# Weight sums of the seven-block products made for two chunks at once, in double-width raw tiles

## The chip, the cores and the metric

The kernel runs on one core of a Trainium2 chip. The metric is the device time of one execution in microseconds (us), as the median of several runs; the profile is one more execution of the same program, taken by the hardware profiler.

## The reference

Two pre-norm residual layers over 512 tokens of width 1024, in float32. Layer 0 has two parallel head groups (grouped-query attention A with per-head normalised and rotated queries and keys, and latent attention B), layer 1 a neighbourhood attention with a relative position bias. A squared-ReLU MLP (1024 to 4096 to 1024) follows each of them.

```python
def hybrid_attention(h, w_in, a_q_norm, a_k_norm, b_q_norm, b_w_uq, b_kv_norm, b_w_ukv, w_out, row, col):
    z = h @ w_in
    qa, ka, va, cq, ckv, kr = jnp.split(z, EVEN_SPLITS, axis=-1)
    qa = axial_rope(rmsnorm(qa.reshape(b, s, A_HEADS, HEAD_DIM), a_q_norm), row, col)
...
    oa = block_attention(qa, ka, va, HEAD_DIM ** -0.5)
    qb = (rmsnorm(cq, b_q_norm) @ b_w_uq).reshape(b, s, B_HEADS, B_NOPE + B_ROPE)
...
    kvb = (rmsnorm(ckv, b_kv_norm) @ b_w_ukv).reshape(b, s, B_HEADS, B_NOPE + B_V)
...
    return mixed @ w_out

def sq_relu_mlp(h, w_up, w_down):
    u = jax.nn.relu(h @ w_up)
    return (u * u) @ w_down
```

## The kernel before, in words

Every product is made of 128 x 128 weight blocks held still in TensorE (PE) while 256 or 512 token columns stream past. A float32 weight is split in two parts, hi (a rounded copy) and lo (the rest), and a product is the sum of three matmuls: hi with the activations' hi, hi with their lo, lo with their hi (lines 515 to 517 for plain products).

**Seven-block products.** Most of the MLPs' up product and part of their down product use a Strassen-like scheme: a 256 x 256 weight square (two k-blocks by two column blocks, 256 KB) is turned into seven 128-wide blocks, and seven half-width products (256 token columns each, three matmuls each, lines 388 to 390) take the place of eight. `seven_chunk` (line 295) makes one such chunk. It takes a free `Slot` of the big pool if more than `reserve` are free, or else one of four raw tiles of 128 x 1024; SP issues one DMA (line 300) into the first 512 columns; GpSimd (POOL) makes three sums (lines 302 to 304) in the columns 512 to 1024; after a `yield`, ScalarE (ACT) copies 896 columns to hi (line 308) and VectorE (DVE) makes lo (line 309). `Seven.plan` asks for the chunks of one group of output columns, and `Seven.run` issues their 21 matmuls each and evacuates four banks (lines 398 to 401, DVE).

**Plain chunks.** `chunk` (line 183) takes one of the four raw tiles, SP loads it (line 190, or 193 for several pieces), ACT makes hi (lines 212 or 222) and DVE or, where `eng` says so, POOL makes lo (line 202). Sweeps of the last layer (`sweep_chunk`, line 288) also fall back to these raw tiles.

**Order.** `weights(i)` keeps chunks loading up to five ahead (`LOAD`) and hi and lo made up to two ahead (`AHEAD`), in the order in which they were asked for. Tiles of a pool tag are handed out in turn, and the one who takes a tile waits for its last reader. A scheduler lays each engine's instructions in an order of its own, which is fixed before the program runs; each engine, and SP's queue of DMAs, goes through its list in order and waits at the head.

**The rope in layer 0's attention.** `rope(..., far=True)` (line 566) swaps partitions with eight DMAs on SP (line 572), multiplies by the cosines and sines on POOL (lines 576, 577), and `sum_q` (line 640) adds both on DVE (line 645), makes hi on ACT (line 647) and lo on DVE (line 648), and issues three more DMAs on SP (lines 649 to 651). Heads' scores (PE, line 1039) wait for these. Beside them run transposes (line 1014) with their copies on ACT and DVE (lines 1016, 1017) and the products with the values (line 1027).

**Bias rows.** `bias_rows` (line 1260) writes the position bias for layer 1 to DRAM: eight loads (line 1264), memsets and copies on POOL (lines 1267 to 1271), and 48 stores on SP (lines 1276, 1280, 1282). It runs as idle work beside the first seven-block stage.

Of the kernel before, what the change touches and what calls it, by code (L numbers as in the profile page):

```python
# [8 lines left out]
F32 = mybir.dt.float32  # L9
# [3 lines left out]
ALU = mybir.AluOpType  # L13
# [5 lines left out]
P = 128  # L19
# [11 lines left out]
def f32(ap):  # L31
    return ap.bitcast(F32)
# [3 lines left out]
def encoder_kernel(ctx: ExitStack, tc: tile.TileContext, ins, out, dbg=None):  # L36
    nc = tc.nc
    PE, ACT, DVE, POOL, SP = nc.tensor, nc.scalar, nc.vector, nc.gpsimd, nc.sync

    big = ctx.enter_context(tc.tile_pool(name="big", bufs=1))  # L40
    wp = ctx.enter_context(tc.tile_pool(name="wp", bufs=3))
# [7 lines left out]
    free = list(range(NSLOT))  # L49
# [11 lines left out]
    def nm(s):  # L61
        cnt[0] += 1
        return f"{s}_{cnt[0]}"
# [116 lines left out]
        return got[0]  # L180


    def chunk(parts, nk, ncol, heads=None, eng=None, first=False):

        raw = wp.tile([P, 1024], F32, tag="raw", bufs=4, name=nm("raw"))
        r3 = raw[:, 0 : nk * ncol].rearrange("p (k n) -> p k n", k=nk)
        for lo, n, src in parts:
            dst = r3[:, :, lo : lo + n]
            if len(src.shape) == 3:
                SP.dma_start(dst, src)  # L190
            else:
                for k in range(nk):
                    SP.dma_start(dst[:, k].rearrange("p (z m) -> p z m", z=src.shape[2]), src[:, k])
        yield
        hi = wp.tile([P, 1024], F32R, tag="whi", name=nm("whi"))
        lo_ = wp.tile([P, 1024], F32R, tag="wlo", name=nm("wlo"))
        m = nk * ncol
        v = lambda t: t[:, 0:m].rearrange("p (k n) -> p k n", k=nk)
        lows = []

        def low(to, src, high):
            z = lambda: (eng or DVE).tensor_tensor(to, src, f32(high), op=ALU.subtract)  # L202
            if eng:
                z()
            else:
                lows.append(z)

        if heads is None:
            if first:
                DVE.tensor_copy(hi[:, 0:m], raw[:, 0:m])  # L210
            else:
                ACT.activation(hi[:, 0:m], raw[:, 0:m], AF.Copy)  # L212
            low(lo_[:, 0:m], raw[:, 0:m], hi[:, 0:m])
        else:

            na, nb = heads
            hn = ncol // (na + nb)
            r4 = r3.rearrange("p k (h e) -> p k h e", h=hn)
            for e0, n, o in ((0, na, 0), (na, nb, hn * na)):
                z = [v(t)[:, :, o : o + hn * n].rearrange("p k (h e) -> p k h e", h=hn) for t in (hi, lo_)]  # L220
                src = r4[:, :, :, e0 : e0 + n]
                ACT.activation(z[0], src, AF.Copy)
                low(z[1], src, z[0])
        yield v(hi), v(lo_), lows

    def rows(w, k0, nk):
        return w[k0 * P : (k0 + nk) * P, :].rearrange("(k p) n -> p k n", p=P)
# [5 lines left out]
    def plan(*spec, make=None):  # L233
        asked.append((make or chunk, spec))
        return len(asked) - 1
# [56 lines left out]

    reserve = [1]

    def seven_chunk(w, k0, c0):


        slot = Slot(F32) if len(free) > reserve[0] else None
        raw = slot.t if slot else wp.tile([P, 1024], F32, tag="raw", bufs=4, name=nm("raw"))
        SP.dma_start(raw[:, 0:512].rearrange("p (k n) -> p k n", k=2), rows(w, k0, 2)[:, :, c0 : c0 + 256])  # L300
        r = raw.rearrange("p (b n) -> p b n", n=P)
        POOL.tensor_tensor(r[:, 6], r[:, 0], r[:, 1], op=ALU.subtract)  # L302
        POOL.tensor_tensor(r[:, 4:6], r[:, 2:3].to_broadcast([P, 2, P]), r[:, 0:7:6], op=ALU.add)  # L303
        POOL.tensor_tensor(r[:, 7], r[:, 3], r[:, 5], op=ALU.subtract)  # L304
        yield
        hi = wp.tile([P, 1024], F32R, tag="whi", name=nm("whi"))
        lo = wp.tile([P, 1024], F32R, tag="wlo", name=nm("wlo"))
        ACT.activation(hi[:, 0:896], raw[:, 128:1024], AF.Copy)  # L308
        DVE.tensor_tensor(lo[:, 0:896], raw[:, 128:1024], f32(hi[:, 0:896]), op=ALU.subtract)  # L309
        if slot:  # L310
            slot.free()
        yield hi, lo, []

    class Seven:
# [56 lines left out]
                s_.free()  # L371

        def plan(self, w, c0, k0=0):
            return [plan(w, k0 + 2 * kp, c0, make=seven_chunk) for kp in range(self.np)]

        def run(self, ids, evac):

# [38 lines left out]
    def product(w, k0, xk, cols, evac, banks=None, kstep=2, stride=None, eng=None, order=None):  # L416
# [13 lines left out]
        for kk in range(0, nk, kstep):  # L430
            n = min(kstep, nk - kk)
            if len(runs) > 1 and stride:
                src = w[(k0 + kk) * P : (k0 + kk + n) * P, :].rearrange("(k p) (z m) -> p k z m", p=P, m=stride)
                parts = [(0, ncols, src[:, :, 0 : len(runs), runs[0][1] : runs[0][1] + runs[0][2]])]
            else:
                src = rows(w, k0 + kk, n)
                parts = [(o, m, src[:, :, c : c + m]) for o, c, m in runs]
            ids.append(plan(parts, n, ncols, None, eng))
# [294 lines left out]
    def load_w(k):  # L733
        _, (hi, lo, lows) = chunk([(0, 768, rows(w_in, k, 1)[:, :, 0:768])], 1, 768, first=k == 0)
        for z in lows:
            z()
        W[k] = hi, lo
# [142 lines left out]
    def projB(g, last):  # L880
        Q, K, V = (QKV[g][z] for z in "QKV")
        iq = [plan([(0, 384, rows(w_uq, 0, 2)[:, :, 384 * g : 384 * g + 384])], 2, 384, (64, 32), POOL),
              plan([(0, 384, rows(w_uq, 2, 1)[:, :, 384 * g : 384 * g + 384])], 1, 384, (64, 32), POOL)]
        iv = plan([(0, 512, rows(w_ukv, 0, 2)[:, :, 512 * g : 512 * g + 512])], 2, 512, (64, 64), POOL)

# [402 lines left out]
    def sweep_chunk(w, k0, kind, made):  # L1288

        def raw():  # L1290
            slot = Slot(F32) if len(free) > reserve[0] else None
            return slot, slot.t if slot else wp.tile([P, 1024], F32, tag="raw", bufs=4, name=nm("raw"))

        def half(k, f):
            return w[k * P : (k + 1) * P, S * f : S * f + S]

        sa, a = raw()
        sb, b = raw() if kind == 2 else (None, None)
        if kind == 0:
            for z in range(2):  # L1300
                SP.dma_start(a[:, S * z : S * z + S], half(k0 + z, 0))
        else:
            for z in range(2):
                SP.dma_start(a[:, S * z : S * z + S], made(z, (z, 1 - z)[kind - 1]))
        if kind == 2:
            SP.dma_start(b[:, 0:S], half(k0 + 1, 1))
        yield
        hi = wp.tile([P, 1024], F32R, tag="whi", name=nm("whi"))
        lo = wp.tile([P, 1024], F32R, tag="wlo", name=nm("wlo"))
        ACT.activation(hi, a, AF.Copy)  # L1310
        DVE.tensor_tensor(lo, a, f32(hi), op=ALU.subtract)
        third = None
        if kind == 2:
            third = Slot()
            ACT.activation(third.t[:, 0:S], b[:, 0:S], AF.Copy)
            DVE.tensor_tensor(third.t[:, S:], b[:, 0:S], f32(third.t[:, 0:S]), op=ALU.subtract)
        for s_ in (sa, sb):
            if s_:
                s_.free()
        yield (hi, lo, third), None, []  # L1320
# [690 lines left out]
```

## Time and profile before

| what | value |
|---|---|
| median of 3 runs | 1179.63 us (1177.93 to 1180.22) |
| the profiled execution's own time | 1178.83 us |
| its span, first to last instruction | 1176.9 us |
| mean granted TensorE clock | 0.998 |
| busy: PE, DVE, ACT, POOL | 1150.5, 902.3, 655.6, 514.1 us |

Every duration below comes from the one profiled execution. "L302" is line 302 of the kernel before. A row of the timeline gives start, duration, engine, line, operation, output and inputs, and in brackets the idle time before it with what ended it. Rows of DMA issues (SPq) give the time that SP was busy with issuing, not that of the transfer. The names in_ev and in_od are weights of layer 0 and of layer 1, in_ffn those of both MLPs; raw, whi, wlo are the tiles of a chunk. "a" is a slot of the big pool, "sc" a scratch tile.

### The profile page before, as it was taken

How to read it: one execution, taken by the hardware profiler on the slowest of the kernel's cores; microseconds unless marked ns; L12 is line 12 of the kernel's file. 1: busy time of each engine (PE TensorE's matmuls, PEld its weight loads, DVE VectorE, ACT ScalarE, POOL GpSimd, SP SyncE). 2: the span in 40 equal slices, each digit the busy share in tenths (PEclk: the TensorE clock that was granted, in tenths of full speed). 3: DMA queues.
4: the chain of work that ended last, by engine and by line, in shares of the span. 5: the costliest groups of instructions: out<-in, count | busy, mean ns of one | idle time of the engine just before them, and what ended most of it. 6: DMA issues, size and time to landing. Idle time of an engine off the chain costs nothing.

```text
span 1176.9 us, 20495 instructions
## 1 busy us (share of the span) xinstructions
PE 1150.5 (98%) x7380; PEld 1024.7 (87%) x7380; DVE 902.3 (77%) x1565; ACT 655.6 (56%) x1116; POOL 514.1 (44%) x658
## 2 busy tenths in 40 slices
PE   9988999999999999999999999999999999999997
PEld 8657778888889899998998989988888999999995
DVE  4788998888977458878795676666898887699855
ACT  5467676664526246672463555555562666676625
POOL 3267444223682376828911333332179998300000
PEclk9999999999999999999999999999999999999999
DMA  7234344433645853435536775655345323375802
GB/s 245 66 94 127 87 126 106 137 79 110 184 130 134 257 177 98 135 101 163 160 72 163 185 172 150 167 146 147 119 109 161 90 82 91 99 250 172 268 1 72
DMA packets 120117, 159.78 MB, mean 136 GB/s; under 512 B 10884, under 2 KB 84529, under 8 KB 119665
## 3 DMA queue, kind: packets, MB, share of 16 engines
q1 hardware_dynamic: 109920, 127.95, 36.0%
q0 software_dynamic: 8640, 17.85, 8.9%
q10 hardware_dynamic: 1456, 12.69, 3.4%
q8 instruction: 58, 0.95, 0.3%
q14 instruction: 43, 0.34, 0.1%
HBM read 136.03 MB, written 29.36 MB: 141 GB/s over the span
## 4 chain that ended last, share of the span: by engine, by line
PE 82%; DVE 4%; ACT 1%; issue 1%; POOL 0%; DVEq 0%; ACTq 0%; POOLq 0%
PE mm L515 7%; PE mm L516 7%; PE mm L517 7%; PE mm L390 3%; PE mm L389 3%; PE mm L388 3%; PE t L389 2%; PE t L388 2%; PE t L390 2%; PE s L516 2%; PE s L517 2%; PE s L515 2%; PE s L390 2%; PE s L388 2%; PE s L389 2%; PE s L1039 1%
## 5 line engine op out<-in xcount | busy, mean ns | idle before, releaser
L309 DVE TENSOR_TENSOR wlo<-a,whi 128x896 fp32r<-128x896 f32 x116 | 149.3, 1291 | 63.0 <-ACT whi L308 62.4
L308 ACT ACTIVATE whi<-a 128x896 fp32r<-128x896 f32 x116 | 109.8, 949 | 127.1 <-PE o L516 41.3
L515 PE MATMUL mm<-a,whi 128*128 128x512 f32 x443 | 178.7, 405 | 0.6 <-DVE a L957 0.4
L517 PE MATMUL mm<-a,wlo 128*128 128x512 f32 x443 | 174.5, 395 | 0.4 <-DVE wlo L202 0.3
L516 PE MATMUL mm<-a,whi 128*128 128x512 f32 x443 | 174.6, 394 | 0.0
L202 DVE TENSOR_TENSOR wlo<-raw,whi 128x1024 fp32r<-128x1024 f32 (+4 forms) x103 | 122.7, 1195 | 48.3 <-ACT whi L212 45.9
L212 ACT ACTIVATE whi<-raw 128x1024 fp32r<-128x1024 f32 (+3 forms) x106 | 101.4, 959 | 86.8 <-PE s L516 29.4
L302 POOL TENSOR_TENSOR a<-a 128x128 f32<-128x128 f32 x116 | 76.8, 665 | 98.4 <-DMA a<-in_ffn_w_up_dram 73.0
L304 POOL TENSOR_TENSOR a<-a 128x128 f32<-128x128 f32 x116 | 106.7, 922 | 8.9
L303 POOL TENSOR_TENSOR a<-a 128x256 f32<-128x256 f32 x116 | 97.4, 843 | 8.9
L517 PEld LDWEIGHTS mm<-a,wlo 128*128 128x128 f32 x443 | 83.1, 188 | 19.5 <-DVE wlo L202 1.1
L515 PEld LDWEIGHTS mm<-a,whi 128*128 128x128 f32 x443 | 83.3, 188 | 18.1 <-DVE hT L973 0.6
L516 PEld LDWEIGHTS mm<-a,whi 128*128 128x128 f32 x443 | 83.5, 188 | 15.1
L390 PE MATMUL mm<-a,wlo 128*128 128x256 f32 x330 | 92.7, 281 | 0.0
L389 PE MATMUL mm<-a,whi 128*128 128x256 f32 x330 | 92.6, 281 | 0.0
L388 PE MATMUL mm<-a,whi 128*128 128x256 f32 x330 | 92.5, 280 | 0.0
L1047 POOL TENSOR_SCALAR p<-p,ti 128x512 f32<-128x512 f32 x64 | 46.9, 735 | 88.0 <-DVE ti L1046 68.9
L1709 POOL TENSOR_SCALAR p<-p,ti 128x256 f32<-128x256 f32 x64 | 35.5, 566 | 97.8 <-DVE ti L1708 85.6
L389 PE MATMUL t<-a,whi 128*128 128x256 f32 x232 | 65.2, 281 | 0.0
L388 PE MATMUL t<-a,whi 128*128 128x256 f32 x232 | 65.1, 281 | 0.0
L390 PE MATMUL t<-a,wlo 128*128 128x256 f32 x232 | 65.0, 280 | 0.0
L390 PEld LDWEIGHTS mm<-a,wlo 128*128 128x128 f32 x330 | 62.1, 188 | 0.3 <-DVE wlo L309 0.2
(403 smaller groups left out, 3566.1 us busy)
## 6 DMA issues: line engine op xcount, KB each, us to landing
a<-in_ffn_w_up_dram SPq DMA_DIRECT2D x101, 256.0 KB
raw<-in_ffn_w_down_dram SPq DMA_DIRECT2D x32, 512.0 KB
made<-in_ffn_w_down_dram ACTq DMA_DIRECT2D x22, 512.0 KB
a<-made SPq DMA_DIRECT2D x38, 256.0 KB
raw<-in_od_w_qkv_dram SPq DMA_DIRECT2D x64, 128.0 KB
a<-in_ffn_w_down_dram SPq DMA_DIRECT2D x29, 256.0 KB
raw<-in_ffn_w_up_dram SPq DMA_DIRECT2D x12, 512.0 KB
raw<-in_ffn_w_down_dram SPq DMA_DIRECT2D x24, 256.0 KB
```

Source lines behind the costliest of these rows:

```text
L202: z = lambda: (eng or DVE).tensor_tensor(to, src, f32(high), op=ALU.subtract)
L212: ACT.activation(hi[:, 0:m], raw[:, 0:m], AF.Copy)
L303: POOL.tensor_tensor(r[:, 4:6], r[:, 2:3].to_broadcast([P, 2, P]), r[:, 0:7:6], op=ALU.add)
L304: POOL.tensor_tensor(r[:, 7], r[:, 3], r[:, 5], op=ALU.subtract)
L308: ACT.activation(hi[:, 0:896], raw[:, 128:1024], AF.Copy)
L309: DVE.tensor_tensor(lo[:, 0:896], raw[:, 128:1024], f32(hi[:, 0:896]), op=ALU.subtract)
L388: PE.matmul(o, wh, x[:, 0], start=kp == 0 and n in (0, 1, 3, 5), stop=False, skip_group_check=True)
L389: PE.matmul(o, wh, x[:, 1], start=False, stop=False, skip_group_check=True)
L390: PE.matmul(o, wl, x[:, 0], start=False, stop=kp == self.np - 1, skip_group_check=True)
L515: PE.matmul(o, wh, xh, start=first, stop=False)
L516: PE.matmul(o, wh, xl, start=False, stop=False)
L517: PE.matmul(o, wl, xh, start=False, stop=last)
```

## The change

Two things change in how raw tiles are used. The ring of four raw tiles of 128 x 1024 becomes one of three of 128 x 2048. A pair of seven-block chunks shares one: at its first chunk both DMAs are issued, and the three sums are made for both at once, at 2 x 128, 2 x 256 and 2 x 128 columns; hi and lo are still made per chunk. Seven-block chunks no longer use slots. Where a plan has five chunks (the down product of layer 0's MLP), the pairs are 2, 2 and 1. Plain chunks and the sweeps' fall-back take halves of such tiles (six halves for four tiles); a half left over is given up when a pair begins. The scratch for DMAs that POOL issues is halved to 8192 bytes to make room.

There are 124 seven-block chunks; their 372 sums become 64 x 3 = 192 (60 for two chunks, 4 for one). The numbers of PE's, DVE's, ACT's and SP's compute instructions and transfers stay as they are.

```diff
+    spare = []
+
+    def raw_pair():
+        return wp.tile([P, 2048], F32, tag="raw", bufs=3, name=nm("raw"))
+
+    def raw_half():
+        if not spare:
+            t = raw_pair()
+            spare.extend((t[:, 0:1024], t[:, 1024:2048]))
+        return spare.pop(0)
+
     def chunk(parts, nk, ncol, heads=None, eng=None, first=False):
-        raw = wp.tile([P, 1024], F32, tag="raw", bufs=4, name=nm("raw"))
+        raw = raw_half()
...
-    def seven_chunk(w, k0, c0):
-        slot = Slot(F32) if len(free) > reserve[0] else None
-        raw = slot.t if slot else wp.tile([P, 1024], F32, tag="raw", bufs=4, name=nm("raw"))
-        SP.dma_start(raw[:, 0:512].rearrange("p (k n) -> p k n", k=2), rows(w, k0, 2)[:, :, c0 : c0 + 256])
-        r = raw.rearrange("p (b n) -> p b n", n=P)
-        POOL.tensor_tensor(r[:, 6], r[:, 0], r[:, 1], op=ALU.subtract)
-        POOL.tensor_tensor(r[:, 4:6], r[:, 2:3].to_broadcast([P, 2, P]), r[:, 0:7:6], op=ALU.add)
-        POOL.tensor_tensor(r[:, 7], r[:, 3], r[:, 5], op=ALU.subtract)
+    def seven_chunk(w, k0, c0, n, z, box):
+        if z == 0:
+            spare.clear()
+            box.append(raw_pair())
+            for q in range(n):
+                SP.dma_start(box[0][:, 1024 * q : 1024 * q + 512].rearrange("p (k n) -> p k n", k=2),
+                             rows(w, k0 + 2 * q, 2)[:, :, c0 : c0 + 256])
+            r = box[0][:, 0 : 1024 * n].rearrange("p (q b n) -> p q b n", q=n, n=P)
+            POOL.tensor_tensor(r[:, :, 6], r[:, :, 0], r[:, :, 1], op=ALU.subtract)
+            POOL.tensor_tensor(r[:, :, 4:6], r[:, :, 2:3].to_broadcast([P, n, 2, P]), r[:, :, 0:7:6], op=ALU.add)
+            POOL.tensor_tensor(r[:, :, 7], r[:, :, 3], r[:, :, 5], op=ALU.subtract)
         yield
+        raw = box[0][:, 1024 * z : 1024 * z + 1024]
...
-            return [plan(w, k0 + 2 * kp, c0, make=seven_chunk) for kp in range(self.np)]
+            boxes = [[] for _ in range(0, self.np, 2)]
+            return [plan(w, k0 + 4 * (kp // 2), c0, min(2, self.np - 2 * (kp // 2)), kp % 2, boxes[kp // 2],
+                         make=seven_chunk) for kp in range(self.np)]
...
-            return slot, slot.t if slot else wp.tile([P, 1024], F32, tag="raw", bufs=4, name=nm("raw"))
+            return slot, slot.t if slot else raw_half()
...
-    nc = _bacc.Bacc("TRN2", target_bir_lowering=False, num_devices=1)
+    nc = _bacc.Bacc("TRN2", target_bir_lowering=False, num_devices=1, dynamic_dma_scratch_size=8192)
```

Since the tiles are handed out otherwise, the scheduler lays the engines' lists otherwise. (Line numbers after are 11 to 14 higher for the same instruction.) In the seven-block stages PE's order is the same; it differs in layer 0's attention, at about 99 to 128 us. SP's list there before: the three DMAs of one query tile's rope (L649 to L651), a plain chunk of w_ukv, the eight swaps of the next tile (L572), a chunk of w_out, then the next three.

```order
L649 DMA a_622<-a_622 64x512
L650 DMA a_622<-sc_746 64x512
L651 DMA a_622<-sc_746 64x512
L190 DMA raw_1059<-in_ev_b_w_ukv_dram 128x2x512
L572 DMA sc_872<-a_126 16x512 x8
L190 DMA raw_1890<-in_ev_w_out_dram 128x2x384
L649 DMA a_871<-a_871 64x512
L650 DMA a_871<-sc_1037 64x512
L651 DMA a_871<-sc_1037 64x512
```

The same place after, with the lines 201, 586 and 663 to 665 for 190, 572 and 649 to 651:

```order
L201 DMA raw_893<-in_ev_b_w_uq_dram 128x2x384
L201 DMA raw_893<-in_ev_b_w_uq_dram 128x384
L201 DMA raw_1050<-in_ev_b_w_ukv_dram 128x2x512
L201 DMA raw_1050<-in_ev_w_out_dram 128x2x384
L663 DMA a_618<-a_618 64x512
L664 DMA a_618<-sc_739 64x512
L665 DMA a_618<-sc_739 64x512
L586 DMA sc_864<-a_126 16x512 x8
L663 DMA a_863<-a_863 64x512
L664 DMA a_863<-sc_1028 64x512
L201 DMA raw_1882<-in_ev_w_out_dram 128x2x384
L665 DMA a_863<-sc_1028 64x512
```

The chunks of w_ukv and w_out now stand ahead of the first tile's three DMAs, and the second tile's swaps follow directly on them; a chunk of w_out now stands between the second tile's last two DMAs.

DVE at the same place before (L1017 copies transposed probabilities, L1043 reduces scores, L645 and L648 are the rope's sum and lo, L872 a lo of other activations):

```order
L1017 TENSOR_TENSOR a_988<-t_989,a_987 128x4x128
L522 SCALAR_TENSOR_TENSOR a_1012<-mm_647,gT,a_1012 128x512
L1043 ISA p_1105,ti_1104<-s_1101,zeros,scA 128x512
L1043 ISA ti_1104 128x1
L991 TENSOR_TENSOR sc_861<-o_931,sc_1004 64x512
L645 TENSOR_TENSOR sc_881<-sc_881,sc_872 128x512
L1046 RECIPROCAL ti_1043<-ti_1043 128x1
L1017 TENSOR_TENSOR a_988<-t_1049,a_987 128x4x128
L872 TENSOR_TENSOR a_1007<-sc_861,a_1007 128x512
L648 TENSOR_TENSOR sc_1037<-sc_881,a_871 128x512
```

And after:

```order
L1031 TENSOR_TENSOR a_980<-t_981,a_979 128x4x128
L536 SCALAR_TENSOR_TENSOR a_1004<-mm_643,gT,a_1004 128x512
L659 TENSOR_TENSOR sc_873<-sc_873,sc_864 128x512
L1005 TENSOR_TENSOR sc_853<-o_923,sc_996 64x512
L1060 RECIPROCAL ti_1034<-ti_1034 128x1
L1057 ISA p_1096,ti_1095<-s_1092,zeros,scA 128x512
L1057 ISA ti_1095 128x1
L662 TENSOR_TENSOR sc_1028<-sc_873,a_863 128x512
L886 TENSOR_TENSOR a_999<-sc_853,a_999 128x512
L1031 TENSOR_TENSOR a_980<-t_1040,a_979 128x4x128
```

The rope's sum comes first, and its lo and the other lo (L662, L886) come ahead of the second copy of transposed probabilities (L1031) instead of behind it.

In the first seven-block stage SP's list had a run of chunk loads and then the position bias (the end of that run here):

```order
L300 DMA a_3930<-in_ffn_w_up_dram 128x2x256
L300 DMA a_3960<-in_ffn_w_up_dram 128x2x256
L300 DMA a_3990<-in_ffn_w_up_dram 128x2x256
L1264 DMA a_4202<-in_od_rpb_dram 16x248 x8
L1282 DMA bx<-a_4204 8x16x128 x3
L1276 DMA bx<-a_4203 8x16x256
L1280 DMA bx<-a_4204 8x16x128
```

After, the stores of the bias stand between the pairs; here from the loads of the fourth pair to those of the fifth:

```order
L312 DMA raw_3648<-in_ffn_w_up_dram 128x2x256 x2
L1290 DMA bx<-a_4146 8x16x256 x4
L1294 DMA bx<-a_4147 8x16x128
L1296 DMA bx<-a_4147 8x16x128
L1294 DMA bx<-a_4147 8x16x128
L1296 DMA bx<-a_4147 8x16x128
L1294 DMA bx<-a_4147 8x16x128
L1296 DMA bx<-a_4147 8x16x128
L1294 DMA bx<-a_4147 8x16x128
L1296 DMA bx<-a_4147 8x16x128
L1290 DMA bx<-a_4146 8x16x256
L312 DMA raw_3748<-in_ffn_w_up_dram 128x2x256 x2
```

Thirteen stores moved in between two pairs' loads.

More of the change, by code (lines that the diff above doesn't have):

```diff
@@ L309, in seven_chunk @@
         DVE.tensor_tensor(lo[:, 0:896], raw[:, 128:1024], f32(hi[:, 0:896]), op=ALU.subtract)
-        if slot:
-            slot.free()
         yield hi, lo, []
```

## The prediction

> **What bounds the kernel now.** I read the page first: busy shares, the row of POOL in the 40 slices, and the chain that ended last.
>
> ```profile
> PE 1150.5 (98%) x7380; PEld 1024.7 (87%) x7380; DVE 902.3 (77%) x1565; ACT 655.6 (56%) x1116; POOL 514.1 (44%) x658
> POOL 3267444223682376828911333332179998300000
> PE 82%; DVE 4%; ACT 1%; issue 1%; POOL 0%; DVEq 0%; ACTq 0%; POOLq 0%
> ```
>
> TensorE holds 82% of the chain that ended last and POOL none of it, although POOL is full in the slices where the seven-block stages lie. So the second view is the windows, one for each stage that the change touches or shifts. A row gives the stretch, its length, then the busy time (and instructions) of PE, its weight loads, DVE, ACT and POOL, then the clock and DMA.
>
> ```profile
> 97.00:126.00 29.00, 25.68 (x142) 18.62 (x141) 23.98 (x54) 22.94 (x51) 20.50 (x23) 1.00 0.37 95
> 142.00:166.00 24.00, 22.57 (x140) 18.35 (x139) 23.46 (x55) 18.90 (x41) 8.59 (x11) 1.00 0.41 110
> 166.00:256.00 90.00, 88.92 (x522) 75.55 (x522) 73.97 (x163) 60.56 (x125) 32.84 (x43) 1.00 0.45 112
> 340.00:380.00 40.00, 40.00 (x337) 39.86 (x336) 29.89 (x35) 23.71 (x31) 16.50 (x23) 1.00 0.43 110
> 424.00:512.00 88.00, 87.07 (x731) 86.37 (x730) 67.59 (x75) 55.16 (x69) 67.65 (x86) 1.00 0.42 108
> 560.00:608.00 48.00, 48.00 (x409) 48.00 (x408) 42.02 (x46) 26.45 (x36) 28.81 (x34) 1.00 0.40 103
> ```
>
> In the three seven-block stretches (340, 424, 560) PE is idle for 0, 0.93 and 0 us. What POOL does there, little or much, costs at most 0.93 us. The idle time of PE lies in layer 0's attention: 3.32 us of 97 to 126, where DVE too idles 5.02 us. After it comes a stretch in which DVE is full (23.46 of 24) and then one in which PE is (88.92 of 90), so time won by both before 126 stays won.
>
> **The sums on POOL.** The groups of the page, busy time and mean:
>
> ```profile
> L309 DVE TENSOR_TENSOR wlo<-a,whi 128x896 fp32r<-128x896 f32 x116 | 149.3, 1291 | 63.0 <-ACT whi L308 62.4
> L308 ACT ACTIVATE whi<-a 128x896 fp32r<-128x896 f32 x116 | 109.8, 949 | 127.1 <-PE o L516 41.3
> L302 POOL TENSOR_TENSOR a<-a 128x128 f32<-128x128 f32 x116 | 76.8, 665 | 98.4 <-DMA a<-in_ffn_w_up_dram 73.0
> L304 POOL TENSOR_TENSOR a<-a 128x128 f32<-128x128 f32 x116 | 106.7, 922 | 8.9
> L303 POOL TENSOR_TENSOR a<-a 128x256 f32<-128x256 f32 x116 | 97.4, 843 | 8.9
> ```
>
> A chunk's three sums take 0.665 + 0.843 + 0.922 = 2.43 us in the mean. One in the timeline runs undisturbed, one beside DVE's L309:
>
> ```profile
> 440.08 0.46 POOL L304 TENSOR_TENSOR a<-a 128x128 f32<-128x128 f32 x1
> 442.62 1.08 DVE L309 TENSOR_TENSOR wlo<-a,whi 128x896 fp32r<-128x896 f32 x1
> 444.27 0.46 POOL L302 TENSOR_TENSOR a<-a 128x128 f32<-128x128 f32 x1 [3.72 <-DMA a<-in_ffn_w_up_dram]
> 444.81 0.74 POOL L303 TENSOR_TENSOR a<-a 128x256 f32<-128x256 f32 x1
> 445.01 1.49 DVE L309 TENSOR_TENSOR wlo<-a,whi 128x896 fp32r<-128x896 f32 x1
> 445.63 1.19 POOL L304 TENSOR_TENSOR a<-a 128x128 f32<-128x128 f32 x1
> ```
>
> 128 columns cost 0.46, 256 cost 0.74: 0.28 for each further 128. Two chunks together then take 0.74 + (0.74 + 2 x 0.28) + 0.74 = 2.78 us undisturbed, against 2 x 1.66 = 3.32 apart. Beside L309 they take 2 x 2.43 = 4.86 now; the excess is 1.54, and I keep half of it, since half as many instructions can be blocked: 3.55 (bounds 2.78 and 4.86). Over 60 pairs POOL gains about 60 x 1.31 = 79 us (bounds 0 and 125). None of it is on the path: TensorE's weights come from L309's lo, not from POOL. It counts only where lo came too late, which is one place; the waits of 463 to 487 hold it (total, times, longest):
>
> ```profile
> PE s L390 <- DVE wlo L309: 0.9, 1, 0.9
> ```
>
> This is the whole 0.93 us of the stage. DVE is late there because L309 takes 1.49 beside a sum and 1.08 alone. Fewer POOL instructions should free a few tenths in every four chunks. I take -0.5, bounds -0.9 (all gone) and 0.
> [...]
>
> **The plain chunks' ring, six halves for four tiles.** This is where I look for the gain. In layer 0's attention SP issues in order, and the rope's eight far swaps (L572) stand behind a chunk that waits for a raw tile:
>
> ```profile
> 84.97 0.46 SPq L651 DMA_DIRECT2D a<-sc  x1
> 89.91 0.37 SPq L190 DMA_DIRECT2D raw<-in_ev_b_w_ukv_dram  x1
> 90.37 6.41 SPq L572 DMA_DIRECT2D sc<-a  x8
> 100.02 1.28 POOL L577 TENSOR_TENSOR sc<-sc,a 128x512 f32<-128x512 f32 x1 [3.22 <-DMA sc<-a]
> 101.34 1.76 DVE L645 TENSOR_TENSOR sc<-sc,sc 128x512 f32<-128x512 f32 x1 [1.11 <-POOL sc L577]
> 103.09 0.67 DVE L1017 TENSOR_TENSOR a<-t,a 128x512 fp32r<-128x512 f32 x1
> 103.68 0.89 DVE L872 TENSOR_TENSOR a<-sc,a 128x512 fp32r<-128x512 f32 x1
> 104.50 0.68 DVE L648 TENSOR_TENSOR sc<-sc,a 128x512 fp32r<-128x512 f32 x1
> 103.81 1.09 PE L1027 MATMUL o<-a,a 128*128 128x256 f32 x7 [1.69 <-DVE a L1017]
> 110.52 1.19 PE L1039 MATMUL s<-a,a 128*128 128x512 f32 x4 [0.70 <-DMA a<-sc]
> ```
>
> SP stood still from 85.43 to 89.91, 4.48 us. The swaps, then POOL's L577, DVE's L645 and L1017, and PE's L1027 wait one behind the other: 3.22, 1.11, 1.69. At the group's end PE waits 0.70 more for L651's product. With six halves the chunk in front is issued before L649 to L651, and L572 follows L651 directly, so the swaps start at about 85.4 and end 4.5 us earlier; L577 then needs no wait (3.22 < 4.5). At stake are 1.69 + 0.70 = 2.39 us of PE. Not all of it goes: in the new order DVE does L645 first, then L648 and L872 ahead of this L1017, 0.68 + 0.89 = 1.57 us more before it, which takes back what L577 and L645 gave (their 1.11 and part of the 3.22), while PE has four more 512-wide products to do in front of L1027 (0.23 apart, 0.93 us of work that need not be done later). And the wait of 0.70 goes, since L648 is done some 2 us sooner. By PE that is 0.93 + 0.70 = 1.63 as the low value; by DVE's idle time 1.11 and what follows it, up to 2.39. I take -2.0; bounds -2.4, and 0 if DVE's order eats it all. What is late next is DVE itself, full from 142.
>
> The third group of swaps stands, in the new order, one chunk further behind (its w_uq chunk waits for a half whose lo POOL makes):
>
> ```profile
> 119.28 1.27 POOL L577 TENSOR_TENSOR sc<-sc,a 128x512 f32<-128x512 f32 x1
> 123.80 0.68 DVE L645 TENSOR_TENSOR sc<-sc,sc 128x512 f32<-128x512 f32 x1
> ```
>
> Between L577's end, 120.55, and L645 there are 3.25 us of cover. I cost it at 0; if that chunk's lo is over 3 us later than before, the excess shows at L645.
> The two waits for halves that now stand between L650 and L651 hold only L651's DMA and the swaps behind; the second group's scores were 0.70 late before and have some 2 us more: 0.
>
> **The seven chunks' ring, three pairs for slots.** Before, a chunk took a free slot and was loaded early; now a pair's two DMAs wait until the second lo of the pair three earlier is made. A chunk is 21 products: 40.00 / 337 x 21 = 2.49 us. From that lo to the first lo of the next user lie 5 chunks, 12.45 us; in the down stage, where a plan has five chunks (pairs of 2, 2 and 1), 4 chunks, 9.96. In that time must fit the DMA, the sums, hi and lo:
>
> ```profile
> 441.52 2.58 SPq L300 DMA_DIRECT2D a<-in_ffn_w_up_dram  x2
> 373.08 0.57 SPq L1276 DMA_DIRECT2D bx<-a  x1
> 373.75 0.40 SPq L300 DMA_DIRECT2D a<-in_ffn_w_up_dram  x1
> 378.38 1.00 POOL L302 TENSOR_TENSOR a<-a 128x128 f32<-128x128 f32 x1 [9.71 <-DMA a<-in_ffn_w_up_dram]
> ```
>
> The DMA: 444.27 - 441.52 = 2.75 us to POOL's start. For the second half I add between 0.40 (SP's issue) and 2.75 (wholly behind the first): 1.6. With the sums 3.55, hi 0.95 and lo 1.29 this is 10.14, bounds 2.75 + 0.40 + 2.78 + 2.24 = 8.17 and 2.75 + 2.75 + 4.86 + 2.24 = 12.6. In the up stages 2.3 us are left over: 0. In the down stage it is 0.2 short, in each of three turns: +0.5, bounds 0 (8.17) and 3 x 2.6 = +8 (12.6).
> The first seven-block stage has a second load: bias_rows' DMAs, 0.57 us of SP each and 0.67 from start to start, stand now between the pairs, thirteen between the fourth and the fifth pair, 13 x 0.67 = 8.7 us against a pair's 4.98. Beside them a chunk's DMA took 378.38 - 373.75 = 4.63 rather than 2.75. At worst that is 8.7 - 4.98 + 1.9 = 5.6 late against 2.3 of slack, +3.3. I take 0, since the first three pairs are loaded before the stage begins and give it six chunks, 14.9 us, of lead.
>
> **Sum.** -2.0 - 0.5 + 0.5 = -2.0, against the profiled execution's own 1178.83 (span 1176.9): 1176.8. That execution lay 0.80 below the median of the runs, 1179.63, from which I count: 1177.6. A measurement of this kernel can tell about 0.2%, 2.36 us, from no change, so the forecast lies just inside that bound.
> The scratch for DMAs that POOL issues is halved as well; no row read here shows one of them (L804) waited for, so 0, and any other value would be a loss.
>
> **Rivals.**
> (a) The loop of three pairs is too short. For it: 10.14 against 9.96 in the down stage, and the bias DMAs. It decides once the second chunk's DMA is over 1.4 us later than the first, with sums of 3.55. Place: PE waiting for L309's lo at about 340 to 380 and 560 to 608. Price: 3.3 in the first stage and 3 x 0.7 in the down stage, in all +5.4 in place of +0.5; with the attention's gain 1179.63 - 2.5 + 5.4 = 1182.5, slower. Against it: the lead at the stage's start, and that PE now waits in neither stretch.
> (b) The attention gives more. DVE idles 5.02 us in 97 to 126; should the later groups of swaps profit as the second does, 4 us go there: 1179.63 - 4.0 - 0.5 + 0.5 = 1175.6. Against it: the third group now stands behind more.
> (c) Nothing happens: DVE's new order gives back all of the attention's gain, POOL's relief is hidden behind PE: 1179.6.
>
> **Chances.** My forecast 0.45, half of it beyond 2.36 us (0.22) and half within (0.23), its own range 1176.0 to 1179.2. (a) 0.27: 0.24 slower, 0.03 within. (b) 0.20, faster. (c) 0.08, within. That makes faster 0.42, same 0.34, slower 0.24. The range goes 1 us past (b) and 1 past (a), 1174.5 to 1183.5; outside are the ends of (a) and of (b), under 2 in 10.
>
> **What would show it.** Right: L572's second group starts at about 85.5, L577 follows without a wait for DMA, PE's waits before L1027 and L1039 at 104 and 110 shrink by 2 us in sum; POOL's sums come to about 64 x 3 instructions and 200 us; in 424 to 512 PE waits under 0.5 us. Wrong: waits of PE for the lo of seven chunks in 340 to 380 or 560 to 608 (rival a), SP waiting longer ahead of the third swaps, or sums of pairs that cost 4.9 us.

## The result, and the profile after

The changed kernel takes 1191.73 us in the median (5 runs, 1187.66 to 1193.9) against 1180.22 for the kernel before in the same session: a ratio of 1.009, interval 1.0073 to 1.0107. It is slower by about 11 us; 1177.6 was forecast. The profiled execution took 1193.9 us (span 1191.7) and was the slowest of the five; its sums are against the 1178.83 of the profile before.

The page of the kernel after: busy times, POOL's slices and the chain that ended last.

```profile
PE 1156.0 (97%) x7380; PEld 1027.9 (86%) x7380; DVE 898.3 (75%) x1565; ACT 654.1 (55%) x1116; POOL 458.7 (38%) x478
POOL 3258343223553247723650332333056667600000
PE 72%; DVE 7%; DMA 2%; issue 2%; ACT 2%; POOL 1%; SPq 1%; ACTq 0%; DVEq 0%; POOLq 0%
```

POOL did save 55 us, and it bought nothing: the chain now leaves PE more often for VectorE, for ScalarE, for transfers and for SP. The windows of the same stretches, PE's busy time first and the clock third from the end:

```profile
97.00:126.00 29.00, 27.09 (x148) 19.87 (x148) 23.92 (x58) 23.37 (x53) 22.36 (x25) 1.00 0.46 114
340.00:380.00 40.00, 37.03 (x294) 36.21 (x292) 23.86 (x27) 19.77 (x26) 18.54 (x18) 0.96 0.73 209
424.00:512.00 88.00, 85.08 (x688) 83.05 (x687) 68.24 (x73) 51.94 (x66) 59.11 (x49) 1.00 0.48 133
560.00:608.00 48.00, 45.57 (x350) 43.51 (x348) 34.84 (x36) 20.17 (x27) 29.26 (x26) 1.00 0.39 112
```

PE was never idle in 340 to 380 and 560 to 608; now it is for 2.97 and 2.43 us, and it got through 294 and 350 matmuls there instead of 337 and 409. In 97 to 126 it is busier than before, 27.09 against 25.68. To see what each stage is worth I followed the same matmul (counted along PE's list, at places where the list is the same in both) through the two traces:

| time in the kernel before | what lies between | the kernel after is later by | step |
|---|---|---|---|
| 172.8 us | layer 0's attention | 0.15 us | +0.15 |
| 350.8 | plain products | 0.10 | -0.05 |
| 397.7 | first seven-block stage | 6.00 | +5.9 |
| 463.7 | second stage, first half | 6.04 | 0.0 |
| 507.0 | second stage, 465 to 500 | 7.94 | +1.9 |
| 568.9 | plain products | 7.77 | -0.2 |
| 616.6 | down stage | 13.27 | +5.5 |
| 655.8 | start of layer 1's attention | 14.27 | +1.0 |
| 1167.7 | all the rest | 15.05 | +0.8 |

Two stages hold 11.4 of the 15.05 us. The groups of the sums and of hi and lo, after:

```profile
L323 DVE TENSOR_TENSOR wlo<-raw,whi 128x896 fp32r<-128x896 f32 x124 | 166.3, 1347 | 89.7 <-ACT whi L322 89.0
L315 POOL TENSOR_TENSOR raw<-raw 128x256 f32<-128x256 f32 (+1 forms) x64 | 57.9, 904 | 196.7 <-DMA raw<-in_ffn_w_up_dram 119.8
L316 POOL TENSOR_TENSOR raw<-raw 128x512 f32<-128x512 f32 (+1 forms) x64 | 107.8, 1684 | 4.9
L317 POOL TENSOR_TENSOR raw<-raw 128x256 f32<-128x256 f32 (+1 forms) x64 | 75.1, 1174 | 5.0
```

A pair's sums take 0.904 + 1.684 + 1.174 = 3.76 us (3.55 was forecast); VectorE's lo went from 1.291 up to 1.347, not down. POOL's wait for loads went from 73.0 us to 119.8.

**The first stage.** SP's, POOL's, ScalarE's, DVE's and PE's rows around the first stall, and at the end SP's wait from 344 to 348 us (total, times, longest):

```profile
345.24 0.57 SPq L1290 DMA_DIRECT2D bx<-a  x1
346.89 0.94 SPq L312 DMA_DIRECT2D raw<-in_ffn_w_up_dram  x2
353.44 0.89 SPq L312 DMA_DIRECT2D raw<-in_ffn_w_up_dram  x2
353.13 1.58 POOL L315 TENSOR_TENSOR raw<-raw 128x256 f32<-128x256 f32 x1 [8.78 <-DMA raw<-in_ffn_w_up_dram]
356.16 0.73 POOL L317 TENSOR_TENSOR raw<-raw 128x256 f32<-128x256 f32 x1
358.51 0.74 POOL L315 TENSOR_TENSOR raw<-raw 128x256 f32<-128x256 f32 x1 [1.62 <-DMA raw<-in_ffn_w_up_dram]
352.89 1.05 ACT L1205 ACTIVATE a<-a 128x1024 f32<-128x1024 f32 x1
358.37 0.50 ACTq L824 DMA_DIRECT2D made<-in_ffn_w_down_dram  x1
359.88 0.93 ACT L322 ACTIVATE whi<-raw 128x896 fp32r<-128x896 f32 x1
343.09 1.46 DVE L323 TENSOR_TENSOR wlo<-raw,whi 128x896 fp32r<-128x896 f32 x1 [1.45 <-ACT whi L322]
360.84 1.50 DVE L323 TENSOR_TENSOR wlo<-raw,whi 128x896 fp32r<-128x896 f32 x1 [6.74 <-ACT whi L322]
360.86 0.39 PE L402 MATMUL mm<-a,whi 128*128 128x256 f32 x1 [1.32 <-ACT whi L322]
362.40 0.38 PE L404 MATMUL mm<-a,wlo 128*128 128x256 f32 x1 [1.03 <-DVE wlo L323]
SPq L312 <- DMA bx<-a: 1.0, 1, 1.0
```

The tile of the fifth pair was free with the lo that ends at 344.55. SP was in the thirteen bias stores until 345.81, waited 1.0 us more for one of them to land, and issued the pair's loads at 346.89, 2.3 us late. Beside the stores the two loads took 6.24 us to POOL's start at 353.13; without stores one load had been seen to take 2.75, and the prediction had 4.35 for two. The sums ended at 356.89. ScalarE could have made hi then, but it stood from 353.94 to 358.37 in front of a copy inside DRAM (line 824), and went on when the sixth pair's load landed, at 358.35. The copy doesn't read that load: in the trace it waits for semaphore 111, on which both the load and the copy signal their end. SP's 1.0 us has the same form, with semaphore 100, a store (landed at 346.82) and the fifth pair's first load. lo was done at 362.34; PE had been waiting since 359.54 (360.86 - 1.32).

**The down stage.** A turn of the ring there, rows of DVE, SP, POOL, ScalarE and PE:

```profile
585.81 2.18 DVE L323 TENSOR_TENSOR wlo<-raw,whi 128x896 fp32r<-128x896 f32 x1
572.03 31.44 SPq L312 DMA_DIRECT2D raw<-in_ffn_w_down_dram  x12
591.44 1.56 POOL L315 TENSOR_TENSOR raw<-raw 128x256 f32<-128x256 f32 x1 [2.10 <-DVE acc L545]
593.08 2.01 POOL L316 TENSOR_TENSOR raw<-raw 128x512 f32<-128x512 f32 x1
595.17 0.74 POOL L317 TENSOR_TENSOR raw<-raw 128x256 f32<-128x256 f32 x1
595.94 1.80 ACT L322 ACTIVATE whi<-raw 128x896 fp32r<-128x896 f32 x2 [4.24 <-POOL raw L317]
596.93 1.20 DVE L323 TENSOR_TENSOR wlo<-raw,whi 128x896 fp32r<-128x896 f32 x1 [1.60 <-ACT whi L322]
598.05 0.41 DVE L414 TENSOR_TENSOR a<-a,mm 128x256 f32<-128x256 f32 x1
598.49 0.69 DVE L415 TENSOR_TENSOR a<-a,s 128x512 f32<-128x512 f32 x1
599.22 1.22 DVE L1588 TENSOR_TENSOR hT<-hT,a 128x1024 f32<-128x1024 f32 x1
600.36 2.17 DVE L323 TENSOR_TENSOR wlo<-raw,whi 128x896 fp32r<-128x896 f32 x1
602.58 0.38 PE L404 MATMUL s<-a,wlo 128*128 128x256 f32 x1 [1.68 <-DVE wlo L323]
```

The lo that gives the tile back ends at 587.99 (585.81 + 2.18), and the first lo of the next user of the tile at 598.13: 10.14 us. (The bracket of POOL's first row names DVE's L545, which the sums don't read; what they need is the load.) The second lo ends at 602.53, since the evacuation (L414, L415) and the addition to the residual (L1588), 2.3 us, came between them and lo itself took 2.17 beside a wide sum. From second lo to second lo it is 14.5 us for five chunks, of which PE uses up one in 2.49, 12.45. PE waits for what is missing.

### The profile page after: what moved, and what is told of

The parts are those of the page before. It is cut to its first block, busy times and chain, and to the rows that moved or that the text cites. A ratio compares the mean times of both kernels' runs of the same rounds, so it can differ in the third digit from the quotient of the medians.

```text
span 1191.7 us, 20193 instructions
## 1 busy us (share of the span) xinstructions
PE 1156.0 (97%) x7380; PEld 1027.9 (86%) x7380; DVE 898.3 (75%) x1565; ACT 654.1 (55%) x1116; POOL 458.7 (38%) x478
## 4 chain that ended last, share of the span: by engine, by line
PE 72%; DVE 7%; DMA 2%; issue 2%; ACT 2%; POOL 1%; SPq 1%; ACTq 0%; DVEq 0%; POOLq 0%
PE mm L529 7%; PE mm L530 7%; PE mm L531 7%; DVE wlo L323 3%; PE mm L404 2%; PE mm L402 2%; PE mm L403 2%; PE s L530 2%; PE s L531 2%; PE s L529 2%; PE s L1053 1%; PE o L1041 1%; PE t L402 1%; PE t L403 1%; PE t L404 1%
## 5 line engine op out<-in xcount | busy, mean ns | idle before, releaser
L323 DVE TENSOR_TENSOR wlo<-raw,whi 128x896 fp32r<-128x896 f32 x124 | 166.3, 1347 | 89.7 <-ACT whi L322 89.0
L322 ACT ACTIVATE whi<-raw 128x896 fp32r<-128x896 f32 x124 | 116.5, 947 | 138.7 <-PE o L530 41.2
L213 DVE TENSOR_TENSOR wlo<-raw,whi 128x1024 fp32r<-128x1024 f32 (+4 forms) x103 | 119.1, 1160 | 48.1 <-ACT whi L223 47.7
L315 POOL TENSOR_TENSOR raw<-raw 128x256 f32<-128x256 f32 (+1 forms) x64 | 57.9, 904 | 196.7 <-DMA raw<-in_ffn_w_up_dram 119.8
L316 POOL TENSOR_TENSOR raw<-raw 128x512 f32<-128x512 f32 (+1 forms) x64 | 107.8, 1684 | 4.9
L317 POOL TENSOR_TENSOR raw<-raw 128x256 f32<-128x256 f32 (+1 forms) x64 | 75.1, 1174 | 5.0
```

Of the source, the lines that this page charges most:

```text
L316: POOL.tensor_tensor(r[:, :, 4:6], r[:, :, 2:3].to_broadcast([P, n, 2, P]), r[:, :, 0:7:6], op=ALU.add)
L317: POOL.tensor_tensor(r[:, :, 7], r[:, :, 3], r[:, :, 5], op=ALU.subtract)
```

## The experiments

Theory 1: the ring of three pairs is too short, because loads that wait for it come late (behind other transfers in SP's list, or because a turn takes longer than PE's use of it). Theory 2: contention, wide sums on POOL hold up VectorE's lo. Theory 3, for the first stage: ScalarE's wait in front of its copy. Each kernel was timed against the kernel before on the same chip; none leaves work out. "Lost at" is read as in the table above, along PE's list against the profile of the kernel before.

**e1: one sum per chunk, in the pair ring.**

```diff
-            POOL.tensor_tensor(r[:, :, 6], r[:, :, 0], r[:, :, 1], op=ALU.subtract)
...
+            for q in range(n):
+                r = box[0][:, 1024 * q : 1024 * q + 1024].rearrange("p (b n) -> p b n", n=P)
+                POOL.tensor_tensor(r[:, 6], r[:, 0], r[:, 1], op=ALU.subtract)
...
```

> The changed kernel with its pair tiles and pair loads, but three sums per chunk as before (372 sums instead of 192). Theory 1 (the ring of three pairs is too short: loads start late, whatever the sums cost): the stall in the first seven-block stage (about 5.9 us by 390 us against the kernel before) stays at 4 us or more, since there the load, not the sum, is late; the down stage keeps 2 us or more of its 4.6; median 1186 to 1192. Theory 2 (contention: wider sums on POOL hold DVE's lo up, 1.347 us in the mean against 1.291): lo goes back to about 1.29, the losses at 465 to 500 (2.3 us) and in the down stage go to under 0.5 each, the first stage keeps its 5.9; median about 1184.

1193.28 us, ratio 1.0115 (1.0089 to 1.0142). Mean lo fell to 1.254 us, and the time did not. Lost at 351 to 398: 7.4; at 465 to 500: 0.0, as theory 2 had it; at 569 to 617: 4.8. The two large losses are not in the width of the sums.

**e2: the plain chunks' halves alone.** `seven_chunk` as before the change, with `raw_half()` for the raw tile where no slot is free; halves and the smaller scratch stay.

> Only the other half of the change: six halves and the smaller scratch for plain chunks; seven-block chunks take slots and are summed one by one as before (and fall back to a half). If the loss is wholly in the seven-block chunks' ring and sums: within 3 us of the kernel before, 1177 to 1181, and layer 0's attention shows SP issuing the second group of swaps right behind the first tile's three transfers. If the smaller scratch or the halves cost something by themselves: 1184 or more.

1180.78 us, ratio 1.0001 (0.999 to 1.0011): halves and scratch cost nothing and gain nothing that the medians show. In its profile it is 1.33 us ahead at 173 us, and loses 0.6 at 465 to 500 and 2.0 after 602.

**e4: the position bias one product earlier.**

```diff
                     if z == 0:
                         later(c, i)
+                        next(bias, None)
                     elif z == 1:
```

> The changed kernel with the position bias's loads and stores asked for one plain product earlier, so that they are issued before the first seven-block stage begins. Theory 1 with the stores as its trigger: the loss of 5.9 us at 354 to 385 goes to under 1.5; the losses at 465 to 500 and in the down stage stay; median 5 us lower than the changed kernel, about 1186. If the loop is too short without the stores: the first stage keeps 3 us or more.

1185.74 us, ratio 1.005 (1.0034 to 1.0067). The first stage's loss went from +5.9 to -0.2: PE is busy for all of 340 to 380. The down stage still loses 6.2. So the pair ring by itself carries the up stages, and it was the stores between its loads that broke it.

**e5: the copies inside DRAM from POOL** (`ACT.dma_start` becomes `POOL.dma_start` in `SumsAhead.steps`).

> The changed kernel with ScalarE's 22 copies of down weights inside DRAM (line 824) issued by POOL instead of ScalarE. Theory 3 (in the first stage ScalarE stood 4.4 us in front of such a copy, which waited for a transfer of the next pair, while the raw for its hi had been ready for 3 us): the first stage's loss falls from 5.9 us to 2 or less; median about 4 us lower than the changed kernel. If theory 1 alone holds there, the loss stays at 4 or more.

1187.17 us, ratio 1.0055 (1.0035 to 1.0075). The first stage still lost 4.25 us. The ninth chunk now came in time, and PE waited for the tenth instead (1.17 us) and once more before 371.6 (1.62). The 1.6 us less than the 5.9 are no more than what a fall of the clock costs (some 1.5 us, last section), which the profile after has in this stage and this one has not. So theory 3 isn't shown to be worth anything by itself. The rest of what this kernel is faster by was won in layer 0's attention, where it was 4.5 us ahead at 173 us: not expected, and looked into with e9.

**e7: six single halves.** The kernel of e2 with `slot = None` in `seven_chunk`.

> The kernel of e2 (six halves, single loads, single sums) with slots taken away from the seven-block chunks: each takes one half of the ring. The ring is as deep as the changed kernel's (six chunks), but a half comes free with its own lo and is loaded alone. Theory 1a (depth: six chunks ahead are too few): loses as much as e1, first stage 5 us or more, down stage 3 or more, median 1188 to 1193. Theory 1b (pairing: a tile is given back only with its second lo, and both loads and all sums come at once, so four chunks of lead remain of six): first stage 3 us or less, down stage under 1; median 1180 to 1184.

1185.6 us, ratio 1.0067 (1.0042 to 1.0092), in neither range. The five times go from 1185.19 to 1190.8, and the profile is of the longest, with a fall of the clock in the first stage (last section). In it, lost at 351 to 398: 6.5; in the down stage 3.3. So the first stage can lose as much with single chunks as with pairs: pairing isn't needed for it, the ring's depth and the order on SP are enough. In the down stage pairs cost some 2 us more than singles do (5.5 against 3.3). That is theory 1a, with 1b for a part of the down stage, in this one execution; where the executions of 1185 us lost their time, no profile shows.

**e8: e4, and the down chunks in slots.**

```diff
+            if self.np % 2:
+                return [plan(w, k0 + 2 * kp, c0, make=one_chunk) for kp in range(self.np)]
             boxes = [[] for _ in range(0, self.np, 2)]
```

> The kernel of e4 (position bias earlier) with the down product's 20 seven-block chunks loaded one by one into free slots and summed one by one, as before the change; the up product's 104 chunks stay in pairs with double-width sums. If the down stage's loss in e4 (6.2 us at 569 to 617) is the ring's: it goes under 0.7, and the median comes to about 1179 (e4's 1185.7 less 6). If it comes from what the up stages leave behind or from the contention of wide sums, 3 us or more stay.

1182.37 us, ratio 1.0025 (1.0011 to 1.0038). The down stage's loss went from 6.2 to 0.4, and PE is busy for all of 560 to 608. Both losses are gone and the median is still 2 us above the kernel before.

**e14: the inverse, only the down chunks in pairs.** The kernel of e2 with `pair_chunk` for plans of five chunks.

> The kernel of e2 with only the down product's 20 seven-block chunks in pairs (2, 2 and 1) of the ring with wide sums; the 104 up chunks stay in slots. The inverse of e8. If the ring of three pairs is enough by itself to stall the down stage: 4 to 6 us lost between 569 and 617 us and nothing at 350 to 510, median 1184 to 1187. If the loss needs what the up stages' ring leaves behind: under 2 us, median 1180 to 1182.

1185.87 us, ratio 1.0048 (1.0029 to 1.0067). Nothing lost at 339 to 464, 1.9 at 465 to 500 (where nothing was expected), 5.9 at 569 to 617. The ring of three pairs stalls the down stage by itself.

The windows of the two stages show both, PE's busy time of 40 and of 48 us. First of e4, then of e8, then of e14:

```profile
340.00:380.00 40.00, 40.00 (x330) 39.45 (x329) 31.53 (x37) 25.23 (x32) 19.02 (x16) 1.00 0.67 190
560.00:608.00 48.00, 43.99 (x365) 43.04 (x364) 38.23 (x40) 21.72 (x30) 33.52 (x30) 1.00 0.45 124
```

```profile
340.00:380.00 40.00, 40.00 (x333) 39.57 (x332) 31.49 (x36) 24.75 (x32) 19.70 (x17) 1.00 0.63 186
560.00:608.00 48.00, 48.00 (x411) 48.00 (x410) 40.91 (x46) 25.91 (x35) 28.41 (x32) 1.00 0.43 115
```

```profile
340.00:380.00 40.00, 40.00 (x338) 39.90 (x337) 28.44 (x34) 23.72 (x30) 17.00 (x24) 1.00 0.42 110
560.00:608.00 48.00, 45.17 (x368) 43.95 (x366) 36.22 (x38) 20.99 (x28) 33.25 (x29) 1.00 0.42 125
```

**e13: e8 with one sum per chunk.**

> The kernel of e8 (position bias earlier, down chunks in slots, up chunks in pairs) with the up chunks' sums made one chunk at a time: 312 sums instead of 156 there. It tells the width of the sums apart from the ring where the ring costs nothing. Theory 2 (wide sums hold VectorE's lo up): lo falls from about 1.33 to 1.25 us in the mean and the time by 0.5 us or more at 430 to 510. Theory 'POOL saves': the time rises by 0.5 or more. If the width is hidden: within 1.5 us of e8.

1181.45 us, ratio 1.0013 (1.0004 to 1.0023), against e8's 1.0025 (1.0011 to 1.0038): no difference that can be told. Here is lo in 424 to 512, of e8 (wide) and of e13 (single):

```profile
L323 DVE TENSOR_TENSOR wlo<-raw,whi 128x896 fp32r<-128x896 f32 x34 | 46.5, 1374 | 16.1 <-ACT whi L322 15.9
```

```profile
L324 DVE TENSOR_TENSOR wlo<-raw,whi 128x896 fp32r<-128x896 f32 x34 | 43.4, 1280 | 18.2 <-ACT whi L323 18.1
```

Theory 2 is right that wide sums hold lo up, by 0.09 us each, and wrong about its price: at 432 to 507 e13 lost 1.1 us and e8 0.6.

**e12: e2 with the bias earlier.**

> The kernel of e2 (six halves for plain chunks, seven-block chunks in slots with single sums) with the position bias earlier, as in e4. It is e8 without pairs. If the wide sums are worth anything by themselves, this is slower than e8's 1182.4; if they are worth nothing, it is equal or faster. By the profiles of e2 and e4 up to 350 us (1.3 and 2.0 us ahead of the kernel before): 1178 to 1181.

1179.39 us, ratio 0.9996 (0.9986 to 1.0006). It is e8 without pairs, and its interval lies wholly below e8's. The pairs cost something beyond the two stalls, and wide sums gain nothing.

**e9, e11, e10: the copies from POOL** in the kernel before, in e2 and in e8.

> The kernel before with ScalarE's 22 copies inside DRAM issued by POOL, nothing else. e5's profile was 4.5 us ahead of the kernel before at 173 us, where the changed kernel's was 0.15 behind. If that comes from ScalarE no longer standing in front of its copies in layer 0's attention: 2 to 4 us faster, 1176 to 1178. If it needs the six halves too: within 1 us of 1180.

> The kernel of e2 (six halves for plain chunks, slots and single sums for seven-block chunks) with the copies issued by POOL. If the two act on different waits of the attention: 3 to 5 us faster than the kernel before, about 1176. If they are the same wait: as e9. If POOL, which is full in 424 to 512 with single sums, makes sums late by its 0.8 us per copy: a loss of 1 to 3 us at 465 to 500.

> The kernel of e8 with ScalarE's copies inside DRAM issued by POOL. e9 and e11 were 2.0 to 2.4 us ahead of the kernel before at 173 us and e5 4.5, but lost it in 430 to 510, where POOL was full of single sums. With wide sums POOL has room there: if that was the cause, the lead of 2 to 4.5 us is kept to the end of the up stage and the median is 1177 to 1180; if the copies compete with the loads, 1 to 2.5 us go there again and it is 1180 to 1183.

e9 1180.16 us, ratio 1.0001 (0.9987 to 1.0014); e11 1183.03, 1.0024 (1.0009 to 1.0038); e10 1180.07, 1.0001 (0.9991 to 1.0011). The lead of 2.4, 2.0 and 4.1 us at 173 us is real in each profile and is given back: by e9 1.9 us, by e11 4.2 and by e10 1.9 at 432 to 507, so POOL's room there (e10's wide sums leave some) does not decide it; e10 lost 1.7 more at 617 to 656. Why is open. That e10 (and e5) led by some 2 us more than e9 and e11 is for the most part the clock: it fell at 75 us in e9 and e11 (mean 0.997 in both profiled executions) and not in e5 and e10 (0.998; last section). No version was faster than the kernel before by more than the measurement can tell.

## Why the prediction was wrong

- **The mechanism was its rival (a), at twice its price.** Rival (a), the loop of three pairs, was given a chance of 0.27 and 5.4 us, in the two places where it struck. It cost 5.9 + 5.5 = 11.4 in the profile. The step of the forecast's own sum that failed is the ring of three pairs, which it put at 0 in the first stage and at +0.5 in the down stage.
- **"In the down stage it is 0.2 short, in each of three turns: +0.5."** This term was 5.5 us (5.9 in e14, alone). The chain came out as forecast, 10.14 us in the turn shown, but by luck: the load took 3.45 us to POOL's start instead of 4.35, and the sums 4.47 instead of 3.55. The mistake is where it ended, at the first lo of the next user, while the tile comes back only with the second. Between them lie the evacuation and the residual's addition on DVE, which the sum left out. The stretch to count was five chunks, 12.45 us, against 14.5.
- **"I take 0, since the first three pairs are loaded before the stage begins."** It cost 5.9; e4 shows that the stores cost it. The lead did carry PE through eight chunks: the last of them had its lo at 354.11, and PE took it up at 356.91. It could not help the fifth pair, whose load waits for a lo that is made two chunks ahead of PE and no earlier. Here the lead in raw tiles was lost at the first turn of the ring. The worst case, 3.3, was too low too, although it had the load right (2.75 + 1.6 + 1.9 = 6.25, and 6.24 was measured). ScalarE's wait in front of line 824, the fall of the clock (some 1.5 us, below) and the stores between the later pairs weren't in it; e5, which had neither of the first two in this stage, still lost 4.25.
- **The attention, "-2.0".** In the profile after, the swaps started at 86.91 behind L665 (90.37 before), L591 did not wait, and PE's waits at 104 and 110 came to 0 and 0.61:

```profile
86.91 7.51 SPq L586 DMA_DIRECT2D sc<-a  x8
98.47 1.30 POOL L591 TENSOR_TENSOR sc<-sc,a 128x512 f32<-128x512 f32 x1
104.22 0.98 PE L1041 MATMUL o<-a,a 128*128 128x256 f32 x7
108.84 0.74 PE L1053 MATMUL s<-a,a 128*128 128x512 f32 x2 [0.61 <-DMA a<-sc]
```

  So the step itself was right, up to the 0.61 that stayed, and it was worth about half of the forecast. Along PE's list from 95.0 to 172.8 us the profile after gains 1.2 us on the kernel before (from 1.37 behind to 0.15), and those of e1, e2, e4, e7, e8, e12, e13 and e14 gain 0.5 to 1.3. The 1.37 that the profile after had to make good come from the fall of its clock at 76 (below). e2's ratio of 1.0001 says that the gain does not reach the end as one that can be measured.
- **"-0.5" at 465 to 500** came out as +1.9 in this profile. Wide sums did not relieve lo, which took 1.374 us in e8 (wide) against 1.280 in e13 (single). But the stall itself isn't settled: of the kernels with single sums e1 lost 0.0 there, e2 0.6 and e14 1.9, the last two with the same instructions up to that place, so it varies from one execution to the next.
- **POOL's 79 us saved, off the path:** 55 us, and off the path it was; e8 against e12 shows no use of it. The sums took 240.8 us in all; the "200 us" among the prediction's signs is less than its own 3.55 us a pair gives (60 x 3.55 + 4 x 2.43 = 223).

What stays open: e8 is some 2 us above the kernel before with both stalls gone, and the one profile of it (1180.48 us, below its median) doesn't show where. About 1 us at 617 to 656 is lost in nearly every profile here, e9's too, so it speaks of the one profile of the kernel before as much as of the change.

## What to carry to other kernels

Size a ring by its whole turn: from the instruction that gives a tile back to the same instruction of the next user, with all that the engines do in between, evacuations too, against the time in which the consumer uses up what the ring holds (here 14.5 us against 12.45). Loads that had been early enough to stand anywhere in the queue became late here, by 2.3 us, as soon as they waited for that ring, and the stores between them then counted (5.9 us in the first stage; -0.2 in e4, which issued them earlier). Sparing POOL 55 us, when it held 0% of the chain, was worth nothing; the buffers that paid for it were worth 11 us.

## What the hardware showed that was not expected

The granted clock was halved twice in the profile after (0.50 in the rows below), for 3.41 us each time, behind a stretch in which PE had been idle for the most part. The windows of the profile after, with the falls in the second and the fourth row:

```profile
72.71:76.12 3.41, 1.19 (x5) 0.96 (x6) 3.08 (x11) 1.99 (x4) 0.00 (x0) 1.00 0.55 186
76.12:79.54 3.42, 3.42 (x10) 2.65 (x9) 2.00 (x7) 1.83 (x6) 0.69 (x1) 0.50 0.00 0
359.43:362.84 3.41, 1.06 (x6) 0.74 (x6) 2.00 (x2) 3.41 (x6) 1.89 (x2) 1.00 0.86 279
362.84:366.26 3.42, 3.42 (x18) 3.42 (x17) 3.42 (x6) 0.96 (x2) 0.44 (x1) 0.50 0.47 153
```

Then two of the kernel before, one of e7 (behind which the clock fell) and one of e2 (behind which it did not):

```profile
70.46:73.88 3.42, 2.03 (x9) 1.31 (x7) 3.13 (x9) 2.46 (x3) 1.43 (x1) 1.00 0.61 205
73.88:77.29 3.41, 2.46 (x11) 1.91 (x12) 3.27 (x8) 2.00 (x5) 0.00 (x0) 1.00 0.00 0
```

```profile
374.82:378.23 3.41, 1.47 (x10) 1.27 (x11) 2.65 (x3) 3.41 (x6) 3.25 (x5) 1.00 1.00 351
```

```profile
73.25:76.67 3.42, 1.60 (x7) 1.28 (x8) 3.16 (x10) 1.91 (x5) 0.00 (x0) 1.00 0.40 136
```

Matmuls of 256 columns start 0.12 us apart at full clock and 0.21 apart from 362.8 to 366.3, which costs some 1.5 us and is a part of the first stage's 5.9. The first fall costs as much: along PE's list the profile after goes from 0.10 to 1.65 us behind in it.

Both falls lasted 3.41 us, and they lie 286.72 us apart, 84 times 3.413. All the changes of the clock in this trace stand in such steps: the first is at 4.45 us, and those at 76.12, 79.54, 362.85, 366.26 and 1185.46 lie 21, 22, 105, 106 and 346 steps behind it; the two of the kernel before, at 5.61 and 1172.97, lie 342 apart. PE had not been idle for the whole of the steps in front of the two falls: it was busy for 1.19 and 1.06 us of them.

The kernel before has the same wait of PE at 72 to 75 us (2.35 us, 2.34 after) and kept its clock. Counted in steps of 3.413 us from the first change of its clock, at 5.61, an edge between two steps lay at 73.88, inside the wait, and PE was busy for 2.03 and 2.46 us of the two. So counted in the profiles before and after, the clock, once full, fell behind every step of which PE was busy for 1.19 us or less and behind none with 1.73 or more; of the rows above, e7's (1.47 us, a fall) and e2's (1.60, none) lie between. (PE's busy time is that of the profile, which models the ends of matmuls.) These counts suggest, and don't prove, that where the steps of an execution lie decides whether the same wait costs 1.5 us: in seven of the 14 profiles here the clock fell between 73.6 and 76.2 us (the kernel after, e1, e7, e9, e11, e12, e14; mean clock 0.995 to 0.997), in the others not (0.998). Over the five runs of the kernel after, the mean clock parts the times into two groups as well: 1187.66 and 1188.08 us at 0.996 and 0.999, 1191.73 to 1193.9 at 0.993 to 0.995.
